# Loads and stores in halves of a tile in a softmax kernel with two DMA queues

## The chip, the cores and the metric

The kernel runs on one core of a Trainium2 chip. The metric is the device time of one execution in microseconds (us). Most figures below are the median of several runs. Runs are classed as fast or slow by their own spread, and ratios use fast runs alone.

## The reference

The kernel computes a softmax over the last axis of 16 x 256 rows of 32,768 float32 numbers, 537 MB in and 537 MB out.

```python
def reference(logits, temperature):          # temperature is 1.0
    scaled = logits / temperature
    scaled = scaled - scaled.max(axis=-1, keepdims=True)
    exp_scaled = np.exp(scaled)
    return (exp_scaled / exp_scaled.sum(axis=-1, keepdims=True)).astype(np.float32)
```

## The kernel before

Each row is split over two partitions, so a tile is 128 partitions x 16,384 columns: 64 KB per partition, 8.4 MB. There are 64 tiles and three buffers, 192 KB per partition. Every piece of a tile is exponentiated with its own maximum; a combination over pieces and over the two partitions of a row then gives one factor per piece, and VectorE (DVE) and ScalarE (ACT) scale the tile in place.

```python
_LOAD = 16384
_PIECES = (4096, 4096, 4096, 2048, 2048)     # maximum and exponential
_ON_DVE = (4096, 4096, 2048, 0, 0)           # columns that DVE scales; ACT the rest
...
    def load(t):
        n = _END if t in (0, G - 1) else _LOAD       # _END = 4096
        for s in range(0, W, n):
            nc.sync.dma_start(out=buf[t % _BUFS][:, s : s + n], in_=x[t * P : (t + 1) * P, s : s + n])

    def store(t, a, b):
        engine = nc.sync if t >= G - 2 else nc.scalar
        engine.dma_start(out=o[t * P : (t + 1) * P, a:b], in_=buf[t % _BUFS][:, a:b])
...
    def normalise(t):
        for k in range(K):
            nc.vector.tensor_reduce(...)             # minus the maximum of piece k
            nc.scalar.activation(... Exp ...)        # in place, with its sum
            ...                                      # tile 0 is stored inside tile 1
        ...                                          # combination: factors f
        for k in range(K):
            ...                                      # scale on DVE and ACT
            if t == G - 1:
                store(t, a, c)
        if 0 < t < G - 1:
            store(t, 0, W)
...
        for t in range(G):
            normalise(t)
            if t and t + _BUFS - 1 < G:
                load(t + _BUFS - 1)
```

SyncE (SP) issues loads, ACT issues stores: those are the two hardware queues, q1 and q10. A load waits until its buffer has been stored.

## Time and profile before

| | before |
|---|---|
| median of three runs | 2496.47 us (2496.07 to 2497.04) |
| span of the profiled run | 2496.7 us |
| busy: DVE, ACT | 63%, 55% |
| DMA engines busy | every slice of the span |
| data rate over the span | 430 GB/s |

The page, the waits, the timeline of a tile and the windows are shown with the prediction. One more view: the DMA issues of the middle tiles (tensors, queue, count, median us from issue to landing).

```profile
x<-in_logits_dram SPq DMA_DIRECT2D x62, 43.7
out_dram<-x ACTq DMA_DIRECT2D x62, 44.5
```

A transfer alone would need about 19.4 us (8.39 MB at 433 GB/s). With two queues sharing the DMA engines it needs twice that, 38.7 us; the rest is time in which it stands behind an earlier transfer of its own queue. The trace also has a record of every DMA packet (queue, size, start, duration). A record doesn't name its DMA engine; where one engine is spoken of below, packets were strung together by their times. The prediction's budget is worked out from these, and so are the tables below; they are my sums over records, not a view.

### The profile page before, as it was taken

The page shows a single profiled execution, that of the slowest core. Times are in us where ns is not written, and L with a number is a line of the kernel's source. Part 1 is how long each engine was busy: PE and PEld are TensorE (multiplying, and loading weights), DVE is VectorE, ACT ScalarE, POOL GpSimd, SP SyncE. Part 2 cuts the span into 40 slices and gives each one's busy share as a digit, 9 for nine tenths or more (in the row PEclk, how much of TensorE's full clock was granted, in tenths as well). Part 3 has the DMA queues.
Part 4 walks back from the last instruction along what each step waited for, and adds up shares of the span by engine and source line. Part 5 has one row for each costly group of instructions (what it writes and reads, how often), then busy time and mean ns, then how long its engine had stood idle before and what let it go on. Part 6 is the DMA issues. An engine that isn't in the chain of part 4 may idle for free.

```text
span 2496.7 us, 2616 instructions
## 1 busy us (share of the span) xinstructions
DVE 1575.6 (63%) x1216; ACT 1367.8 (55%) x895; POOL 0.2 (0%) x4
## 2 busy tenths in 40 slices
DVE  6576665766657656576565665656657566565665
ACT  6464654645546455464554645546455464554655
POOL 0000000000000000000000000000000000000000
DMA  9999999999999999999999999999999999999998
GB/s 419 436 429 430 433 437 436 435 437 426 434 434 437 433 426 435 434 436 423 433 433 433 435 425 436 436 433 425 435 422 436 421 437 436 421 436 422 436 429 380
DMA packets 19748, 1073.91 MB, mean 430 GB/s; under 512 B 2192, under 2 KB 2192, under 8 KB 2192
## 3 DMA queue, kind: packets, MB, share of 16 engines
q1 hardware_dynamic: 10800, 553.65, 51.4%
q10 hardware_dynamic: 8928, 520.10, 48.4%
q14 instruction: 20, 0.16, 0.0%
HBM read 536.87 MB, written 536.87 MB: 430 GB/s over the span
## 4 chain that ended last, share of the span: by engine, by line
DMA 73%; DVE 16%; ACT 9%; another core or an unknown queue 2%; issue 0%; SPq 0%; DVEq 0%; ACTq 0%
DMA x<-in_logits_dram 37%; DMA out_dram<-x 36%; DVE nm L101 12%; ACT x L108 7%; DVE x L140 3%; ACT x L144 2%; DVE f L136 0%; ACT ee L121 0%; DVE rS L135 0%; DVE Sh L80 0%; DVE ttj L124 0%; DVE Sh L77 0%; SPq L62 0%; DVEq L189 0%
## 5 line engine op out<-in xcount | busy, mean ns | idle before, releaser
L101 DVE TENSOR_REDUCE nm<-x 128x1 f32<-128x4096 f32 x318 | 1117.5, 3579 | 683.8 <-DMA x<-in_logits_dram 683.8
L108 ACT ACTIVATE x<-x,nm 128x4096 f32<-128x4096 f32 x318 | 965.4, 3036 | 1025.3 <-DVE nm L101 1025.3
L144 ACT ACTIVATE x<-x,f 128x2048 f32<-128x2048 f32 (+1 forms) x194 | 370.9, 1975 | 74.0 <-DVE f L136 74.0
L140 DVE TENSOR_SCALAR x<-x,f 128x4096 f32<-128x4096 f32 (+2 forms) x194 | 372.2, 1975 | 2.5 <-DVE f L136 0.2
L124 DVE CUSTOM_DVE_ANT_0 ttj<-ee,ssum 128x5 f32<-128x5 f32 (+1 forms) x64 | 10.6, 166 | 196.7 <-ACT ee L121 196.7
L108 ACT ACTIVATION_READ_ACCUMULATOR x<-x,nm 128x1 f32 x318 | 59.2, 186 | 0.0
L121 ACT ACTIVATE ee<-nm,nMh 128x5 f32<-128x5 f32 (+1 forms) x64 | 18.1, 284 | 0.0
L136 DVE TENSOR_SCALAR f<-ee,rS 128x5 f32<-128x5 f32 (+1 forms) x64 | 14.8, 231 | 2.2
L135 DVE RECIPROCAL rS<-Sh 128x1 f32<-128x1 f32 x64 | 10.5, 164 | 2.2
L80 DVE TENSOR_TENSOR Sh<-Sh 128x1 f32<-128x1 f32 x64 | 10.2, 159 | 2.2
L80 DVE TENSOR_TENSOR nMh<-nMh 128x1 f32<-128x1 f32 x64 | 10.2, 159 | 2.2
L119 DVE TENSOR_REDUCE nMh<-nm 128x1 f32<-128x5 f32 (+1 forms) x64 | 10.1, 158 | 2.2
L77 DVE STREAM_SHUFFLE Sh<-Sh 128x1 f32<-128x1 f32 x64 | 9.7, 151 | 0.0
L77 DVE STREAM_SHUFFLE nMh<-nMh 128x1 f32<-128x1 f32 x64 | 9.7, 151 | 0.0
L108 ACT ACT_TABLE_LOAD x1 | 1.3, 1283 | 8.1 <-DMA x<-in_logits_dram 8.1
L124 DVE DVE_READ_ACCUMULATOR2_ANT Sh<- 128x1 f32 x64 | 5.2, 82 | 0.0
L77 DVE LOAD_MASK_SELECT Sh<-Sh x64 | 0.9, 14 | 2.8
L77 DVE LOAD_MASK_SELECT nMh<-nMh x64 | 0.9, 14 | 2.8
L175 POOL MEMSET const-uint8-127<- 128x1 uint8 x1 | 0.1, 102 | 0.0
L175 POOL MEMSET const-bfloat16-1.0<- 128x1 bf16 x1 | 0.1, 101 | 0.0
L175 POOL MEMSET const-float32-0.0<- 128x1 f32 x1 | 0.1, 98 | 0.2 <-issue 0.2
L175 POOL MEMSET const-float32-1.0<- 128x1 f32 x1 | 0.1, 98 | 0.0
## 6 DMA issues: line engine op xcount, KB each, us to landing
x<-in_logits_dram SPq DMA_DIRECT2D x8, 2048.0 KB, 23.7
out_dram<-x SPq DMA_DIRECT2D x4, 2048.0 KB, 15.1
x<-in_logits_dram SPq DMA_DIRECT2D x62, 43.7
out_dram<-x ACTq DMA_DIRECT2D x62, 44.5
out_dram<-x SPq DMA_DIRECT2D x1, 29.4
```

Source lines behind the costliest of these rows:

```text
L77: nc.vector.stream_shuffle(out=v[:, j + 1 : j + 2], in_=v[:, j : j + 1], mask=mask)
L80: nc.vector.tensor_tensor(out=v[:, j + 1 : j + 2], in0=v[:, j : j + 1], in1=v[:, j + 1 : j + 2], op=op,)
L101: nc.vector.tensor_reduce(out=nm[:, k : k + 1], in_=xc, axis=X, op=A.max, negate=True)
L108: nc.scalar.activation(out=xc, in_=xc, func=Exp, bias=nm[:, k : k + 1], scale=inv_t, accum_out=ssum[:, k : k + 1],)
L119: nc.vector.tensor_reduce(out=nMh[:, 0:1], in_=nm, axis=X, op=A.min)
L121: nc.scalar.activation(out=ee, in_=nm, func=Exp, bias=nMh[:, n_rounds : n_rounds + 1], scale=-1.0)
L124: nc.vector.tensor_tensor_reduce(out=ttj, in0=ee, in1=ssum, scale=1.0, scalar=0.0, op0=A.mult, op1=A.add, accum_out=Sh[:, 0:1],)
L135: nc.vector.reciprocal(out=rS, in_=Sh[:, n_rounds : n_rounds + 1])
L136: nc.vector.tensor_scalar_mul(out=f, in0=ee, scalar1=rS)
L140: nc.vector.tensor_scalar_mul(out=xs[:, a:b], in0=xs[:, a:b], scalar1=f[:, k : k + 1])
L144: nc.scalar.activation(out=xs[:, b:c], in_=xs[:, b:c], func=Copy, scale=f[:, k : k + 1])
L175: nc = _bacc.Bacc("TRN2", target_bir_lowering=False, num_devices=1)
```

## The change

The intent: hand on half a tile as soon as it is ready, so that both queues always hold work, and shorten the end by smaller last pieces. Transfers of the middle tiles become 8,192 columns wide, 32 KB per partition. The core of the diff:

```diff
-_LOAD = 16384
-_PIECES = (4096, 4096, 4096, 2048, 2048)
-_ON_DVE = (4096, 4096, 2048, 0, 0)
-_END = 4096
-_END_ON_DVE = 2560
+_LOAD = (8192, 8192)
+_PIECES = (4096, 4096, 4096, 4096)
+_ON_DVE = (4096, 1024, 4096, 1024)
+_HALF = 8192
+_FIRST_PIECES = (4096, 4096, 4096, 4096)
+_FIRST_ON_DVE = (2560, 2560, 2560, 2560)
+_LAST_PIECES = (4096, 4096, 4096, 2048, 2048)
+_LAST_ON_DVE = (2560, 2560, 2560, 2048, 0)
 ...
-                store(0, 0, W)
+                for h in range(0, W, _HALF):
+                    store(0, h, h + _HALF)
 ...
             if t == G - 1:
                 store(t, a, c)
-        if 0 < t < G - 1:
-            store(t, 0, W)
+            elif t and c % _HALF == 0:
+                store(t, c - _HALF, c)
```

More of the change, by code (lines that the diff above doesn't have):

```diff
@@ L45 @@
     n_rounds = _SPLIT.bit_length() - 1
-    K = max(len(_PIECES), W // _END)
+    K = max(len(_FIRST_PIECES), len(_PIECES), len(_LAST_PIECES))
     pool = ctx.enter_context(tc.tile_pool(name="fixed", bufs=1))
@@ L57, with cut @@
     ]
+    def cut(t: int) -> tuple:
+        if t == 0:
+            return _FIRST_PIECES, _FIRST_ON_DVE, _FIRST_PIECES
+        if t == G - 1:
+            return _LAST_PIECES, _LAST_ON_DVE, _LAST_PIECES
+        return _PIECES, _ON_DVE, _LOAD
     def load(t: int) -> None:
-        n = _END if t in (0, G - 1) else _LOAD
-        for s in range(0, W, n):
+        s = 0
+        for n in cut(t)[2]:
             nc.sync.dma_start(
@@ L65, in load @@
             )
+            s += n
     def store(t: int, a: int, b: int) -> None:
@@ L88, in normalise @@
         xs = buf[t % _BUFS]
-        if t in (0, G - 1):
-            sizes = [_END] * (W // _END)
-            on_dve = [_END_ON_DVE] * len(sizes)
-        else:
-            sizes, on_dve = _PIECES, _ON_DVE
+        sizes, on_dve, _ = cut(t)
         K = len(sizes)
```

## The prediction

> **What bounds the kernel now.** I read the page from the top: busy shares, the DMA slices, the queues.
>
> ```profile
> DVE 1575.6 (63%) x1216; ACT 1367.8 (55%) x895; POOL 0.2 (0%) x4
> ...
> DMA  9999999999999999999999999999999999999998
> ...
> DMA packets 19748, 1073.91 MB, mean 430 GB/s; under 512 B 2192, under 2 KB 2192, under 8 KB 2192
> ...
> q1 hardware_dynamic: 10800, 553.65, 51.4%
> q10 hardware_dynamic: 8928, 520.10, 48.4%
> q14 instruction: 20, 0.16, 0.0%
> HBM read 536.87 MB, written 536.87 MB: 430 GB/s over the span
> ```
>
> No compute engine is near full. The 16 DMA engines are, in every slice: loads on q1 and stores on q10 together cover 99.8% of the span. So the kernel is bound by moving 1,073.7 MB, each byte once in and once out, which no variant can shrink. Note that two hardware queues are in use already: the change adds none.
>
> Then the waits of the queue that issues loads, and the timeline of one tile (start, duration, engine).
>
> ```profile
> SPq L62 <- DMA out_dram<-x: 2382.1, 61, 78.9
> ...
> 1207.02 0.33 SPq L62 DMA_DIRECT2D x<-in_logits_dram  x1
> 1211.78 4.42 DVE L101 TENSOR_REDUCE nm<-x 128x1 f32<-128x4096 f32 x1 [11.07 <-DMA x<-in_logits_dram]
> ...
> 1240.10 0.34 ACTq L70 DMA_DIRECT2D out_dram<-x  x1
> 1245.69 0.33 SPq L62 DMA_DIRECT2D x<-in_logits_dram  x1
> ```
>
> A load waits for the store that empties its buffer. A tile lands at 1211.8, its store is issued at 1240.1 (28.3 us of compute), and the next load is issued at 1245.7 when the previous store has landed. Loads take a median 43.7 us and stores 44.5 us; 43.7 + 28.3 + 44.5 = 116.5 us is one turn of a buffer, a third of it 38.8 us, the period. These times stretch because the DMA is full; they don't set the period.
>
> How near is it to what the DMA engines can do? Windows of early and late steady running, then of the end (last two columns: DMA share, GB/s):
>
> ```profile
> 60.00:1260.00 1200.00, 754.62 (x584) 653.88 (x431) 0.00 (x0) 1.00 1.00 433
> 1260.00:2460.00 1200.00, 766.95 (x591) 665.36 (x437) 0.00 (x0) 1.00 1.00 431
> ...
> 2465.00:2470.00 5.00, 1.62 (x8) 3.85 (x4) 0.00 (x0) 1.00 0.64 275
> 2470.00:2475.00 5.00, 5.00 (x4) 5.00 (x4) 0.00 (x0) 1.00 0.76 316
> 2475.00:2490.00 15.00, 0.20 (x1) 0.12 (x1) 0.00 (x0) 1.00 0.99 422
> 2490.00:2497.00 7.00, 0.00 (x0) 0.00 (x0) 0.00 (x0) 1.00 0.21 90
> ```
>
> In the trace's packet records (queue, size, start, duration) a whole tile goes as 128 packets of 64 KB, 8 per DMA engine. Their median is 2,418 ns, and the next packet of an engine most often starts 4 ns before the last one ends: a pitch of 2,414 ns, the same for load after store as for load after load. The 16 KB packets of the first and last tile take 611 ns, pitch 607. The small completion packet after each transfer adds about 6 ns.
>
> **The budget of one DMA engine**, from these: 1,000 packets of 64 KB x 2.414 = 2,414.0; 96 of 16 KB x 0.607 = 58.3; 137 completions x 0.006 = 0.8; together 2,473.1 us. The span is 2,496.7, so 23.6 us are lost. Beginning: about 2.6 us before and during the first packets, 1.1 where the first store joins. End: the last data packet ends at 2,495.05, 1.6 us before the end. The remaining 18 us are in the middle and the tail: packets over their 2,418 ns (14.4 us per DMA engine over the run, hardly any before 600 us), instruction fetches (19 of 0.31 us on q14 inside the span), and engines out of step. By 660 us one DMA engine ends each load 7 to 8 us after the first one. The next load is issued only 4.3 to 4.4 us before the last one lands, so on the early engines the load queue runs dry for some 3 us per tile; the one store packet in progress then takes about 0.7 us more on nearly all engines at once (at 1,475.8, 1,982 and 2,255 us it took 2.9 to 3.5 us). At the tail the late engine never idles: the other engines' dip at 2,465 to 2,475 costs the end nothing.
>
> **What the Trainium skill says.** "DMA: Bandwidth & Descriptors", section "Where 436 GB/s comes from", gives a ceiling of 435.2 GB/s. The trace agrees: from 611 to 2,418 ns for 48 KB more is 27.2 GB/s per engine, 435 for 16, and 433 run steadily. The same page, "Issuing engines are not separate DMA queues", says that transfers of different queues interleave on the same 16 engines, so more queues bring no bandwidth; the records agree, q1 and q10 packets alternating one by one. Its "Why small descriptors are slow" names a fixed cost of about 3 cycles per packet; the pitches above leave 607 - 602.3 = 4.7 ns per packet at 27.2 GB/s, of that order.
>
> **The change, part by part.**
>
> *Packets of 32 KB.* Pitch by the line through the two measured sizes: 4.7 + 1,204.7 = 1,209.4 ns, so two cost 4.7 ns more than one of 64 KB. Per engine now 2,000 x 1.2094 = 2,418.8; 80 of 16 KB = 48.6; 32 of 8 KB x 0.306 = 9.8; 264 completions = 1.6; sum 2,478.8. That is **+5.7 us**, wholly on the path.
>
> *Loads in halves, compute starting on the first.* After the second half lands, two maxima of 4.41, the last exponential 3.7 + 0.2, the combination 1.4 and the first half's scaling (2.35 + about 0.75 on DVE beside about 2.85 on ACT) lead to a store: 8.8 + 3.9 + 1.4 + 3.1 = 17.2 us, where it was 28.3. By itself worth nothing, as compute is hidden. But the turn stays near 116 us, so waiting in the queues must grow: the second half is held 20.4 us (17.2 + 3.2), the first about 36 (19.4 for the second half's load, then 17.2), leaving about (116 - 28)/2 = 44 us each for load and store. The service of a half at half rate is only 19.4 us. Each queue then holds more than one further half ahead, about 24 us instead of 4 to 5, more than the 7 to 8 us by which engines differ. The queues should no longer run dry, and the long store packets should mostly vanish: I take 9 to 10 us of the middle's loss as recovered, **-9.5 us**.
>
> *Pieces and split of scaling.* DVE per tile: 4 x 4.41 + 2 x (2.35 + 0.75) + 1.3 = 25.1 us; ACT: 4 x 3.89 + 2 x 2.85 + 0.3 + 2 x 0.34 = 22.2. Both stay well under 38.8. Zero.
>
> *Last tile in small pieces, tile 62 in halves.* The final store is 1 MB, not 2, and tile 62's stores start some us earlier. But the late DMA engine was never idle there, so only a smaller lead of the other engines shows: **-2 us**.
>
> Sum: 2,496.5 + 5.7 - 9.5 - 2 = 2,490.7, say **2,490.5 us**.
>
> **Rivals.** (1) *Packet cost alone*: the long packets have nothing to do with dry queues (refresh, interference) and stay: 2,496.5 + 5.7 - 0 to 2 = 2,500 to 2,502. For it: they are nearly absent at first and come later, which age of the run might explain. Against: they coincide with the end of a load on q1, on almost all engines at once. (2) *Hidden anyway*: smaller packets cost nothing beyond 435 GB/s, and the tail is unchanged; gains and costs cancel: 2,495 to 2,498. (3) *The deeper queues let engines drift further*: a late engine ends the run alone; 2,496 to 2,505. The records show drift levelling off at 8 us just where the queue lead ends, which speaks for this one. (4) *Best case*: all loss but beginning and end (5.3 us) goes: 2,478.8 + 5.3 = 2,484.
>
> **Range and chances.** From the best case to the packet rival: 2,484 to 2,501. A gain of 2% would need 2,446.5, below the floor of 2,473 us that the packet pitch sets: all but excluded. A loss of 2% is 50 us, nine times the packet term; it would take a stall that I don't see, such as the store issue holding up ACT.
>
> **What would show it.** Right: data packets of 32 KB with a median near 1,213 ns; few store packets 0.5 us over their median; loads issued 20 us or more before the previous half lands; DVE waiting for loads still; rate in the late window no lower than in the early one. Wrong: a 32 KB median above 1,220 ns (7 ns x 2,000 = 14 us); DMA share below 0.97 in the steady windows; a wait of ACT or of DVE that ends the run; or the last DMA engine over 10 us behind the others.

## The result, and the profile after

| | before | after |
|---|---|---|
| median of four runs each | 2496.27 us | 2493.20 us |
| lowest and highest | 2493.07 to 2497.04 | 2493.09 to 2494.35 |
| span of the profiled run | 2496.7 us | 2491.5 us |

The ratio is 0.9991 with a 95% interval of 0.9974 to 1.0008: the same within 2%. A ratio is the mean time of one kernel's fast runs over that of the other's of the same rounds, so it isn't quite the ratio of the medians. The interval includes no difference at all, and one of the four runs before took 2493.07 us. The profiled run before took 2498.45 us and is none of the four, so the spans in the table differ by more than the medians do. The changed kernel repeats itself far better: a later set of five runs gave 2492.97 to 2493.19 us, while the kernel before ranged from 2492.0 to 2524.35 beside it.

The page of the changed kernel: busy shares, DMA share by slice, packets, queues (packets, MB, share).

```profile
DVE 1580.1 (63%) x1217; ACT 1352.5 (54%) x711; POOL 0.2 (0%) x4
...
DMA  9999999999999999999999999999999999999998
...
DMA packets 38038, 1073.94 MB, mean 431 GB/s; under 512 B 4224, under 2 KB 4224, under 8 KB 4224
...
q1 hardware_dynamic: 20160, 553.66, 51.6%
q10 hardware_dynamic: 17856, 520.10, 48.4%
q14 instruction: 22, 0.18, 0.0%
```

The same bytes go in twice the packets, and the DMA still binds. Now the waits of the loading queue, two kinds of DMA issue, and the timeline of a tile.

```profile
SPq L72 <- DMA out_dram<-x: 2339.5, 122, 47.8
```

```profile
x<-in_logits_dram SPq DMA_DIRECT2D x124, 4096.0 KB, 31.3
out_dram<-x ACTq DMA_DIRECT2D x124, 4096.0 KB, 49.3
```

```profile
1204.78 8.75 DVE L108 TENSOR_REDUCE nm<-x 128x1 f32<-128x4096 f32 x2 [10.26 <-DMA x<-in_logits_dram]
...
1221.73 0.34 ACTq L81 DMA_DIRECT2D out_dram<-x  x1
...
1225.00 0.34 ACTq L81 DMA_DIRECT2D out_dram<-x  x1
```

The second half lands at 1,204.8, and the first store is issued 17.0 us later, the second 20.2 us later; before it was 28.3 us for the whole. A half needs 19.4 us of service at half rate, so a load of 31.3 us stands about 12 us behind others and a store of 49.3 us about 30. Before, it was about 5 and 6 us. Loads still wait for stores; that is how the full DMA looks from the issuing queue here.

The windows (the last two columns are DMA share and GB/s):

```profile
60.00:1260.00 1200.00, 768.57 (x594) 656.79 (x342) 0.00 (x0) 1.00 1.00 433
1260.00:2460.00 1200.00, 762.37 (x587) 651.31 (x343) 0.00 (x0) 1.00 1.00 433
...
2465.00:2470.00 5.00, 1.18 (x1) 1.97 (x2) 0.00 (x0) 1.00 1.00 423
2470.00:2475.00 5.00, 0.00 (x0) 0.00 (x0) 0.00 (x0) 1.00 0.99 419
2475.00:2490.00 15.00, 0.00 (x0) 0.00 (x0) 0.00 (x0) 1.00 0.57 242
```

The late stretch now runs at 433 GB/s, where it was 431. The dip at 2,465 to 2,475 us is gone, but from 2,483 us on most DMA engines have nothing left.

The budget of one DMA engine, averaged over the 16: every packet at its median duration less the 4 ns overlap, completions at 6 ns, and what is lost in three stretches. "Long" packets are those of 32 or 64 KB that took over 0.3 us more than their median after the first 60 us.

| profiled run | span | packets at their pitch | lost to 60 us | lost 60 to 2,440 | lost after 2,440 | long packets: load, store |
|---|---|---|---|---|---|---|
| before | 2496.7 | 2473.1 | 3.6 | 12.9 | 7.0 | 81, 198 |
| after | 2491.5 | 2477.9 | 3.3 | 2.0 | 8.2 | 9, 3 |

So smaller packets cost 4.8 us, the middle gives 10.9 back, and the end costs 1.2 more: net 5.2 us of span.

What a long packet is, I had not read closely enough. This is one DMA engine of the kernel before, from the packet records (start us, queue, ns, bytes; `issue` is ACT's store instruction):

```
2250.22  q10     9      4     a store completes; nothing else on q10
2250.22  q1   2418  65536
2252.64  q1   2418  65536
2253.07  issue of the next store
2255.05  q1      9      4     the load completes; nothing else on q1
2255.06  q10  3258  65536     first packet of that store
2258.31  q10  2418  65536
```

The long packet is the first of a store issued late, and it comes when **both** queues of this engine have nothing else left. If it took its usual 2,418 ns, it began at 2,255.9, 2.8 us after the issue and 0.8 us after the engine came free. No load could fill the gap: the next one waited for the previous store to land on the latest DMA engine, at 2,258.5, and was issued at 2,258.9. Over the run, 178 of the 198 long store packets are of this kind: the first of a store, right after a load's completion. Together with shorter delays of the same kind they make about 7 of the 12.9 us; the rest is spread over other packets, mostly loads.

### The profile page after: what moved, and what is told of

It reads as the page before. It is cut to its first block, busy times and chain, and to the rows that moved or that the text cites. A ratio compares the mean times of both kernels' runs of the same rounds, so it can differ in the third digit from the quotient of the medians.

```text
span 2491.5 us, 2807 instructions
## 1 busy us (share of the span) xinstructions
DVE 1580.1 (63%) x1217; ACT 1352.5 (54%) x711; POOL 0.2 (0%) x4
## 4 chain that ended last, share of the span: by engine, by line
DMA 68%; another core or an unknown queue 15%; DVE 11%; ACT 4%; issue 1%; SPq 0%; ACTq 0%
DMA out_dram<-x 41%; DMA x<-in_logits_dram 28%; DVE nm L108 8%; ACT x L115 3%; DVE x L148 3%; SPq L72 0%; DVE f L144 0%; ACT x L152 0%; ACT ee L129 0%; DVE rS L143 0%; DVE Sh L91 0%; DVE Sh L88 0%; DVE ttj L132 0%; ACTq L197 0%
## 5 line engine op out<-in xcount | busy, mean ns | idle before, releaser
L108 DVE TENSOR_REDUCE nm<-x 128x1 f32<-128x4096 f32 (+1 forms) x257 | 1119.1, 4395 | 639.0 <-DMA x<-in_logits_dram 639.0
L115 ACT ACTIVATE x<-x,nm 128x4096 f32<-128x4096 f32 (+1 forms) x257 | 949.3, 3694 | 976.4 <-DVE nm L108 976.0
L152 ACT ACTIVATE x<-x,f 128x3072 f32<-128x3072 f32 (+1 forms) x132 | 366.4, 2781 | 129.9 <-DVE f L144 73.5
L148 DVE TENSOR_SCALAR x<-x,f 128x1024 f32<-128x1024 f32 (+3 forms) x256 | 379.9, 1548 | 2.3
L132 DVE CUSTOM_DVE_ANT_0 ttj<-ee,ssum 128x4 f32<-128x4 f32 x64 | 10.4, 162 | 228.2 <-ACT ee L129 228.2
L115 ACT ACTIVATION_READ_ACCUMULATOR x<-x,nm 128x1 f32 x257 | 47.9, 186 | 0.0
L129 ACT ACTIVATE ee<-nm,nMh 128x4 f32<-128x4 f32 x64 | 18.0, 282 | 0.0
L144 DVE TENSOR_SCALAR f<-ee,rS 128x4 f32<-128x4 f32 x64 | 14.7, 229 | 2.2
L127 DVE TENSOR_REDUCE nMh<-nm 128x1 f32<-128x4 f32 x64 | 10.0, 157 | 2.2
## 6 DMA issues: line engine op xcount, KB each, us to landing
x<-in_logits_dram SPq DMA_DIRECT2D x124, 4096.0 KB, 31.3
out_dram<-x ACTq DMA_DIRECT2D x124, 4096.0 KB, 49.3
```

The costliest lines, as they stand in the source:

```text
L108: nc.vector.tensor_reduce(out=nm[:, k : k + 1], in_=xc, axis=X, op=A.max, negate=True)
L115: nc.scalar.activation(out=xc, in_=xc, func=Exp, bias=nm[:, k : k + 1], scale=inv_t, accum_out=ssum[:, k : k + 1],)
L127: nc.vector.tensor_reduce(out=nMh[:, 0:1], in_=nm, axis=X, op=A.min)
L129: nc.scalar.activation(out=ee, in_=nm, func=Exp, bias=nMh[:, n_rounds : n_rounds + 1], scale=-1.0)
L132: nc.vector.tensor_tensor_reduce(out=ttj, in0=ee, in1=ssum, scale=1.0, scalar=0.0, op0=A.mult, op1=A.add, accum_out=Sh[:, 0:1],)
L144: nc.vector.tensor_scalar_mul(out=f, in0=ee, scalar1=rS)
```

## The experiments

Theory, as revised: a DMA engine loses time only where both its queues are empty. That needs a store issued late (compute holds the tile long) and a next load that still waits for a store to land on the latest engine. Rivals: 64 KB packets or the age of the run cause the long packets; compute is hidden and doesn't matter. The expectations of the first four runs were written before this revision, for a load queue that runs dry; the revised form is first put to a test in the two runs with one more maximum. All runs but the probe with cut compute gave correct results.

### The changed kernel again

No edit.

> The changed kernel unaltered, as the yardstick for the other runs on this chip. Both theories: 2491 to 2495 us, ratio 0.997 to 1.000; one DMA engine 7 to 8 us behind at the end, no store packet 0.5 us over its median after the first 60 us.

It took 2493.12 us (2492.97 to 2493.19), ratio 0.9971 (0.9931 to 1.0012). The budget repeats: 2.0 us lost in the middle, 8.1 at the end, 10 and 2 long packets.

### Loads in halves alone

```diff
-_LOAD = 16384
+_LOAD = 8192
```

> The kernel before with its loads in two halves and nothing else: stores stay whole, in 64 KB packets. Theory of the dry queue: the second half is held about 19.5 us instead of 28.3, so the leads of both queues together grow from about 10 to 19 us, more than the 7 to 8 us by which DMA engines differ; the long packets go, at half the packet cost (+2.7 us): span 2473.1 + 2.7 + 5.3 + 7 = 2488, time 2489 to 2491, ratio 0.996 to 0.998. Rival, that long packets come with 64 KB stores or with the age of the run: they stay, 2496 to 2499, ratio 1.000 to 1.001.

It took **2603.84 us** (2582.31 to 2615.61), ratio 1.0406. Both theories missed by 100 us. The issues of this kernel, and a window in its middle:

```profile
x<-in_logits_dram SPq DMA_DIRECT2D x124, 4096.0 KB, 49.2
...
out_dram<-x ACTq DMA_DIRECT2D x62, 35.0
```

```profile
1200.00:1300.00 100.00, 60.92 (x53) 52.24 (x36) 0.00 (x0) 1.00 0.88 372
```

A half load now takes longer, from issue to landing, than a whole store. In the records an engine with both queues full sends one 32 KB load packet (1,213 ns), then one 64 KB store packet (2,418 ns), and so on: loads get a third of the rate. At 1,236 to 1,248 us the load packets of one late engine come 3.63 us apart, the sum of the two, while the others have only stores left. A load counts as landed only when that engine is done too. The DMA share falls to 0.88, and 121 us are lost in the middle (here from 60 us to 57 us before the end). So far this is read from records; the run with equal packets below tests it.

### Stores in halves alone

```diff
-_PIECES = (4096, 4096, 4096, 2048, 2048)
-_ON_DVE = (4096, 4096, 2048, 0, 0)
+_PIECES = (4096, 4096, 4096, 4096)
+_ON_DVE = (4096, 1024, 4096, 1024)
 # and the two edits of the stores from the change; loads and last tile as before
```

> The kernel before with its stores (and pieces of scaling) in halves and nothing else: loads stay whole. Theory of the dry queue: the load can't be used before it has landed whole, the second half is stored 29 us after, the leads together are about 13 us as against 10, so the load queue still runs dry and the long packets stay: 2495 to 2499, ratio 1.000 to 1.001. Rival, that the 64 KB store packet is to blame: they go, 2489 to 2492, ratio 0.997 to 0.998.

It took 2495.25 us (2493.98 to 2496.49), ratio 0.998 (0.9943 to 1.0016), in the range of the theory but too near the rival's to part them by time. The records don't part them either: long store packets fall from 198 to 5, as the rival had it, but 153 long load packets stand where 81 did, and 8.7 us are lost in the middle. Nor does the revised theory cover this run. Each load was issued a median 5.5 us after the previous one had landed, so the load queue ran dry in every middle tile, while stores were issued 17 us or more before the previous one landed. Still the first packet of a load could be long: one, at 1,291.0 us between two packets of a store that was under way, took 2,824 ns. Why is open. Unequal packets the other way round, with loads getting two thirds, cost nothing like the 100 us of the run above.

### Compute cut to a quarter, packets of 64 KB

```diff
-            xc = xs[:, at[k] : at[k] + sizes[k]]
+            part = sizes[k] if t in (0, G - 1) else sizes[k] // 4
+            xc = xs[:, at[k] : at[k] + part]
 # and the same for the scaling of the middle tiles; wrong result on purpose
```

> The kernel before with every compute instruction of the 62 middle tiles cut to a quarter of its columns (a wrong result on purpose; same instructions, same transfers in 64 KB packets). Compute holds a tile about 9 us instead of 28.3, the leads together about 30 us. Theory of the dry queue: no long packets, steady rate 433.6 GB/s, span 2473.1 + 5.3 + 7 = 2485.5, time 2486 to 2488, ratio 0.995 to 0.997. Rival, that compute is hidden and 64 KB packets lose time by themselves: 2495 to 2497, ratio 0.999 to 1.001.

It took 2501.33 us (2494.02 to 2504.89), ratio 1.0001: by the ratio the rival's number. But the steady state did what the theory says. Not one store packet is long, and 3.6 us are lost from 60 to 2,440 us in place of 12.9, with the very same packets. The gain is given back at the end, as the windows show:

```profile
2450.00:2460.00 10.00, 9.08 (x3) 7.90 (x5) 0.00 (x0) 1.00 0.81 352
2460.00:2470.00 10.00, 6.05 (x15) 7.76 (x8) 0.00 (x0) 1.00 0.18 78
```

Stores had fully caught up by then, and the last tile, whose compute I had left at full size, held up everything: 17.4 us lost after 2,440. So packets of 64 KB don't make store packets long by themselves; how long compute holds a tile does. There were still 54 long load packets, where there had been 81.

### Equal packets: loads and stores in halves, stored together

```diff
-_LOAD = 16384
+_LOAD = 8192
 ...
-            store(t, 0, W)
+            for h in range(0, W, _LOAD):
+                store(t, h, h + _LOAD)
 # the same for tile 0; pieces, scaling and last tile as before
```

> The slow kernel with loads in halves, plus its store issued as two halves, both only when the whole tile is done: packets of 32 KB on both queues, pieces, scaling and last tile as before. Theory of unequal packets (queues take turns packet by packet, so 32 KB loads beside 64 KB stores get a third of the rate): the 100 us go, 2491 to 2496 us, ratio 0.997 to 0.999. Rival, that loads in halves are slow by themselves: 2580 to 2615, ratio 1.034 to 1.047.

It took 2493.68 us (2493.58 to 2493.86), ratio 0.9983 (0.997 to 0.9997). The slow kernel differs from this one only in its stores: whole, one 64 KB row per packet, in place of two halves with packets of 32 KB. The issues of this version:

```profile
x<-in_logits_dram SPq DMA_DIRECT2D x124, 4096.0 KB, 31.4
out_dram<-x ACTq DMA_DIRECT2D x124, 4096.0 KB, 48.1
```

The 110 us are gone, so the loss lay in halved loads beside whole stores. Two things go with that, though. In the slow kernel both halves of a load also wait for one whole store and are issued together (at 1,213.5 us, within 0.8 us); here each half follows half a store. How much of the loss is the unequal shares and how much this, no run tells apart. This version also holds nearly all of the change's effect (2.1 us lost in the middle), without the early store and without the new last tile.

### The changed kernel with its old last tile

```diff
-_LAST_PIECES = (4096, 4096, 4096, 2048, 2048)
-_LAST_ON_DVE = (2560, 2560, 2560, 2048, 0)
+_LAST_PIECES = (4096, 4096, 4096, 4096)
+_LAST_ON_DVE = (2560, 2560, 2560, 2560)
```

> The changed kernel with its last tile in four equal pieces, as before. The first store of the last tile comes about 3.8 us later (a 4096-wide maximum and exponential in place of 2048-wide ones), while the halves of the tile before it are still being stored until 5 to 9 us after that store was issued. Theory that the tail was bound by one late DMA engine anyway: cost 0 to 1.5 us, 2493 to 2495. Rival, that the small pieces carry the gain: cost 3 to 5 us, 2496 to 2498.

It took 2493.02 us (2492.86 to 2493.08). The small last pieces are worth nothing.

### More instructions

```diff
+        if 0 < t < G - 1:
+            for _ in range(20):
+                nc.vector.memset(scratch, 0.0)      # one column
```

> The changed kernel with 20 tiny memsets of one column on VectorE per middle tile (1,240 more instructions, 45% more; about 2 us per tile where VectorE idles 10). Theory of instruction fetch: fetches on q14 rise from 22 to about 32, the latest DMA engine falls 7.5 x 32/22 = 10.9 us behind in place of 7.5, and the end comes 3 to 4 us later: 2496 to 2497 us. Rival, that the lateness of three DMA engines has nothing to do with fetches: 2493 to 2494.

The reason for this test is in the changed kernel's records. Thirteen DMA engines end every load within 0.5 us of each other; three fall behind. The latest engine's lag behind the first, beside instruction fetches (8 KB on q14, 0.309 us each):

```
fetch at us              336.0  601.9  873.6  1140.5  1384.6  1650.6  1919.9  2189.4
lag before it, us          1.2    2.0    2.7     3.4     4.2     5.2     5.8     6.7
lag one or two loads on    2.0    2.7    3.4     4.2     5.1     5.8     6.7     7.5
```

Each of these steps of the latest engine's lag follows a fetch. The load packet after a fetch is also recorded longer, mostly 1.46 to 1.78 us in place of 1.21, which makes up the rest of a step. The run with more instructions took 2506.19 us (four fast runs 2505.63 to 2506.24; one slow run of 2560.39), ratio 1.0032. The direction is the theory's, the size nearly four times larger. Its profile fell on the slow run, so only the number of fetches is taken from it:

```profile
q14 instruction: 31, 0.25, 0.0%
```

Whether the fast runs lost the other 9 us because the lag passed the 11.6 us by which loads are issued ahead, no fast profile shows; that stays open.

### Fewer instructions

```diff
-_PIECES = (4096, 4096, 4096, 4096)
-_ON_DVE = (4096, 1024, 4096, 1024)
+_PIECES = (8192, 8192)
+_ON_DVE = (5120, 5120)
```

> The changed kernel with two pieces of 8192 in place of four of 4096 in the middle tiles, scaling split 5120 to 3072: about 8 instructions fewer per tile. Theory of instruction fetch: 22 fetches become about 18, the latest engine 6 us behind, 2491 to 2492.5 us, faster than the changed kernel by about 1.4 us. The store of a half is issued about 3 us later, which the leads should cover. Rival: no change, or slower if the store queue runs dry with the load queue: 2493 to 2497.

It took 2492.24 us (2491.94 to 2492.74), ratio 0.9977 (0.9964 to 0.9991), with 18 fetches. On the same chip the changed kernel with its old last tile took 2493.02, so the gain is about 0.8 us where 1.4 was expected. The end lost 6.8 us in place of 8. The records add something on the theory above: loads were issued only 4.4 us before the previous one landed, as in the kernel before, but stores 32 us or more, and the middle lost just 1.8 us.

### One more maximum per tile, in both kernels

```diff
+        if 0 < t < G - 1:
+            nc.vector.tensor_reduce(out=ttj[:, 0:1], in_=xs[:, W - 4096 : W], axis=X, op=A.max)
         nc.vector.tensor_reduce(out=nMh[:, 0:1], in_=nm, axis=X, op=A.min)
```

In the kernel before:

> The kernel before with one more maximum of 4096 columns per middle tile ahead of the combination (result unused), so that each store is issued 4.4 us later; VectorE stays under 34 of 38.8 us per tile. Theory that a DMA engine loses time when both its queues are empty because the store is issued late: the loss grows, by 4 to 20 us: 2500 to 2517, ratio 1.002 to 1.008. Rival, that compute is hidden behind a full DMA: no change.

It took 2527.3 us (2521.21 to 2531.79), ratio 1.0103 (1.0064 to 1.0143), above the expected range. In the changed kernel:

> The same extra maximum in the changed kernel: stores issued 4.4 us later. Theory: the store queue holds more than that, both queues are never empty at once, no change: 2492.5 to 2494.5 us. Rival, that any lengthening of compute is felt: 2497 or more.

It took 2494.25 us (2493.57 to 2496.75). The same 4.4 us of compute, on engines that stay about 75% busy at most, cost one kernel 1% and the other about 1 us. A window of each, before first:

```profile
60.00:1260.00 1200.00, 879.62 (x615) 652.82 (x428) 0.00 (x0) 1.00 1.00 427
```

```profile
60.00:1260.00 1200.00, 902.22 (x621) 657.60 (x341) 0.00 (x0) 1.00 1.00 433
```

The first has 480 long store packets (415 of them the first of a store, right after a load's completion) and 37.3 us lost in the middle, the second one long store packet and 2.1 us. The DMA share column says 1.00 for both, since the record of a packet seems to include its wait; the rate column tells them apart.

### Quarters

```diff
-_LOAD = (8192, 8192)
+_LOAD = (4096, 4096, 4096, 4096)
-_HALF = 8192
+_HALF = 4096
```

> The changed kernel with loads and stores in quarters of a tile, 16 KB packets. Packet cost from the pitches: 4,000 x 0.607 = 2,428.0 in place of 2,000 x 1.2093 = 2,418.6 us, plus 248 more completions x 0.006 = 1.5, plus one to two more fetches: 10.5 to 13 us over the changed kernel, 2503.5 to 2506.5 us, if the queues stay full. Rival, that packet size costs nothing: 2493 to 2495. More than 2510 would say that a queue runs dry, for instance because transfers wait for one of few completion semaphores.

It took 2505.43 us (2504.79 to 2506.64). The packets at their pitch sum to 2,489.4 us, 11.5 more than in halves, and 3.8 us are lost in the middle. The time is 12.3 us over the changed kernel's 2493.1 (not run in this set), in the expected range, so the cost per packet holds at 16 KB.

### A lean version

```diff
-_PIECES = (4096, 4096, 4096, 4096)
-_ON_DVE = (4096, 1024, 4096, 1024)
+_PIECES = (8192, 8192)
+_ON_DVE = (8192, 8192)
 ...
-        nc.vector.tensor_reduce(out=nMh[:, 0:1], in_=nm, axis=X, op=A.min)
-        combine(nMh, A.min)
+        own_other = both.rearrange("p (q w k) -> p w q k", q=2, w=2)
+        nc.vector.stream_shuffle(out=own_other[:, 1], in_=own_other[:, 0], mask=[i ^ 1 for i in range(32)])
+        nc.vector.tensor_reduce(out=nMh, in_=both[:, 0 : 2 * K], axis=X, op=A.min)
 # exponentials and the sum then run over 2K columns, and combine(Sh, A.add) is gone
```

> The version with fewer instructions taken further: combination by one exchange of maxima and sums together instead of two, all scaling on VectorE; 32 KB packets, halves and last tile as in the changed kernel. Theory of instruction fetch: about 15 fetches in place of 22, the latest DMA engine about 5.5 us behind, 2490.3 to 2491.8 us, the fastest of all; it beats both kernels by 1.5 us or more. Rival: no better than 2492.2, as other losses remain.

It took 2491.4 us (2490.45 to 2492.04), ratio 0.9954 (0.9927 to 0.9981), the fastest of all.

```profile
span 2489.7 us, 1807 instructions
...
q14 instruction: 14, 0.11, 0.0%
```

This set ran on a chip where the kernel before had a median of 2502.47 us. Against the changed kernel (2493.1 to 2493.2 in two sets of rounds, not run in this set) it is about 1.7 us. The end lost 6.5 us in place of 8.2, so a third fewer fetches removed a fifth of it: lateness is not simply proportional.

## Why the prediction was right or wrong

The time, 2493.2 us, lies in the range and 2.7 us above the estimate. The range of 2,484 to 2,501 us also holds the time of the kernel before, so the number alone proves little. Step by step:

- **Packets of 32 KB, +5.7 us.** Right, a little large: the sums differ by 4.8 us in the traces, and the 32 KB packets have the expected median of 1,213 ns. Quarters added 11.5 us, where 10.9 were worked out for packets and completions.
- **Loss of the middle recovered, -9.5 us.** Right in size: 10.9. The working was wrong in one point. I wrote that the load queue runs dry and "the one store packet in progress" takes longer. The packet isn't in progress; it is the first of a late store, and both queues are empty. The probe with cut compute ran without one long store packet although loads were still issued only 4.4 us before the previous one landed: late loads cost little while stores are well ahead. That a dry load queue costs nothing isn't shown. In the probe it was hardly dry: the first DMA engine ended a load a median 1.1 us after the next was issued, where before it ended 2.8 us too early. With stores in halves alone it was dry in every middle tile, and 8.7 us were lost.
- **"About 44 us each for load and store", 24 us ahead.** Wrong split, about the right sum: 31.3 and 49.3 us. Loads are issued 11.6 us before the previous half has landed on the last engine, so the sign "20 us or more" failed; stores are 28 us ahead or more. It was enough, since the lag reached 7.5 us. The early store, on which the 17.2 us rest, was also hardly needed: with equal packets stored together the second half is held 18.2 us, and the middle loses 2.1 us.
- **Held 17.2 and 20.4 us.** Measured 17.0 and 20.2.
- **Tail, -2 us.** Wrong sign: the end lost 1.2 us more, and restoring the old last tile changed nothing. In both kernels the latest DMA engine sets the end: before, one engine was 3.5 us behind the others with its last data; after, three were, the last by 7.5 us. This term is the furthest off, by 3.2 us, but the packet and middle terms erred the other way, and the span of the profiled runs fell by 5.2 us where the terms add up to 5.8. The rest of the 2.7 us is the base: the losses were read off an execution of 2,498.45 us and then taken from a median of 2,496.5. That the terms offset each other so well is luck. (The prediction also counts 19 fetches inside the span; its page has 20.)
- **Rivals.** The packet-cost rival fell with the cut compute: same packets, no long stores. The drift rival was half right. Three engines do end the run alone, 4 to 7.5 us after the others, where before one did, by 3.5 us. In steady running the lag was no larger than before (7.5 us against 7 to 8.7). That late stores held the other engines of the kernel before back to the pace of the slow ones fits the records, but wasn't tested.
- **Not foreseen:** what only half of the change would have done. Loads in halves beside whole stores lose 4%.

Open: why three engines carry the fetches and why the packet after a fetch is longer, so that 0.31 us cost 0.6 to 0.9; what makes load packets long beside a full store queue; what the run with more instructions lost beyond its fetches; why the kernel before varies from 2,492 to 2,524 us. That it issues only a few us ahead would fit, but wasn't tested.

## What to carry to other kernels

When the DMA is the bound, ask of every DMA engine whether its queues always hold work, and read the rate, not the busy share: compute that looks hidden cost 1% where stores were issued late, and about 1 us once transfers were split. Apart from halved loads beside whole stores, the largest losses came where both queues of an engine were empty, but one queue that ran dry beside a full one was not free either (8.7 us in stores in halves alone). Give all queues packets of the same size, and split loads and stores together. When nothing else is left, the engine that also fetches instructions ends the run, and fewer instructions are a small gain.

## What the Trainium skill lacked or had wrong

- "DMA: Bandwidth & Descriptors", "Queues, rings and completion order", says that an engine takes turns between queues packet by packet, but not what follows: each partition's row is one packet here, up to 64 KB, so on an engine with both queues full rates went by row size (a load packet every 3.63 us). Loads of 32 KB beside stores of 64 KB took 2603.8 us, and 2493.7 us with both at 32 KB.
- The same page, "Where 436 GB/s comes from", says that for transfers between HBM and SBUF the HBM side (about 358 GB/s) binds. With one core active, loads and stores together ran at 433 GB/s in both steady windows. The page itself says elsewhere that the figure is a core's share with both cores of a pair streaming; that sentence leaves it out.
- "Runtime: NRT & Kernel Launch", "Instruction fetch mechanics", lacks what fetches cost a DMA that is full. Here fetches of 8 KB on q14 took 0.31 us each, and three of the 16 engines ended 4 to 7.5 us late.
- "Perfetto Trace Analysis", "DMA Engine Tracks", says that the slices show actual busy time. Here a packet's record seems to include its wait: store packets with a median of 2,418 ns were recorded with up to 3,496 ns when both queues had been empty. At 2,255 us fourteen engines began such records, and thirteen of them ended within 0.4 us of each other.
- "DMA: Bandwidth & Descriptors", "Why small descriptors are slow", lacks a measured cost per packet for large packets; the runs show about 4.7 ns at 16 to 64 KB, 11.5 us per DMA engine for twice the packets of the changed kernel.
